# Ten projections turned round: tokens as the stationary operand, 512 columns of weights streaming, and the result turned back by a product with diag(1 / rms)

## The chip, the cores and the metric

The kernel runs on one core of a Trainium2 chip. The metric is the device time of one execution in microseconds (us); smaller is better. Engines: PE is TensorE (its matrix products; PEld is its loading of the stationary operand, which overlaps with them), DVE is VectorE, ACT is ScalarE, POOL is GpSimd, SP is SyncE, whose queue issues nearly all transfers here.

## The reference, cut to what matters

The reference is one block of a flow-matching backbone with two layers on 256 latent tokens (and 256 context tokens) of 2048 channels. Layer 0 mixes tokens with a bidirectional RWKV-7 scan, layer 1 with a Hyena long convolution; after each mixer comes a dense MLP.

```python
for i in range(DEPTH):                       # two layers
    h = modulate(rms_norm(x, norm_g[i, 0]), mod[:, 0], mod[:, 1])
    y = rwkv_mixer(...) if i == 0 else hyena_stream(...)      # last step: ... @ w_o,  ... @ out_w + out_b
    x = x + mod[:, 2] * rms_norm(y, norm_g[i, 1])             # residual 1
    h = modulate(rms_norm(x, norm_g[i, 2]), mod[:, 3], mod[:, 4])
    u = square(relu(h @ mlp_up[i]))                           # 2048 -> 8192
    y = u @ mlp_down[i]                                       # 8192 -> 2048
    x = x + mod[:, 5] * rms_norm(y, norm_g[i, 3])             # residual 2
```

So there are four residuals, and each adds a normalised projection: y times 1 / rms of its token (a number per token), times a gain per channel. The weights that feed them are `w_o` (2048 x 2048), `mlp_down` of layer 0 and of layer 1 (8192 x 2048 each) and `hy_out_w` (2048 x 2048): ten matrices of 2048 x 2048 in all, since the kernel takes `mlp_down` in four parts.

## The kernel before, in words

Activations are held with channels on the 128 partitions and tokens along the row: `x[k]` is 128 channels x 256 tokens, k from 0 to 15. Everything is float32; a product is made from three fp32r products. Each operand is cut into a high part (an ACT cast) and a low part (a DVE subtraction), and `mm3` (lines 158, 159, 160) issues high x high, high x low and low x high into one accumulator in PSUM. In the profile's names `wh`, `wl` are the parts of a weight, `hxh`, `hxl` those of a normalised input of a layer, `uh`, `ul` those of an MLP's hidden values, `yh`, `yl` those of the RWKV mixer's output; `mm` is the accumulator.

`load_split` fetches 1 MB of a weight matrix in one transfer (line 137, queue SP) and cuts it, 1024 columns at a time, with one ACT and one DVE instruction. `gemm_ws` then does a projection with a 128 x 128 block of weights as the stationary operand (the first matrix in a shape such as `128*128 128x256`) and the 256 tokens (258 with two modulation columns) as the moving one. It goes through the output channels two blocks at a time: for each pair, all 16 input blocks k, so 16 x 2 x 3 = 96 products; 8 pairs make 768 products of 256 columns. With `lead=True` the first two pairs run side by side in four accumulators, so that each input block, which is only just being made, is used for four output blocks as soon as it is there.

After a projection `resid` adds it to x. Before, this works on 16 blocks `o[m]` of 128 channels x 256 tokens. While the projection runs, POOL squares each block that comes out and adds it up (`square_sum`, lines 393 to 397). At the end two squares are left to ACT; a product with a matrix of ones sums over the channels (line 370 and 376), ACT takes the root and DVE the reciprocal of a 128 x 256 tile that has the same value in all partitions. Then for each block k: DVE multiplies by gain and 1 / rms into `rt`, DVE (POOL for every fourth block) adds to `x`, ACT scales into `hxh`, DVE makes `hxl`, ACT squares x (`sq`) and PE sums the squares for the next norm (line 376). The next projection (MLP up or Hyena in, both with `lead=True`) consumes `hxh`, `hxl` block by block. The last residual has no next layer: its multiplications and additions are shared between DVE and POOL, and each block goes out by a transfer (line 425).

Beside this the kernel computes the modulation from `ada_w` in the background: transfers into `aw`, and a running sum `acc` made by DVE during the first MLP, by ACT and POOL (line 293) from Hyena on; PE ends each piece with a small product (line 277, `sg<-ones,acc`). A credit counter (`tick`) sets after how many loads of weights such a piece is written into the program. During Hyena's output projection the same counter lets in the spectral part (transposes, `sc` and `sg` products) of the last quarter of the channels, which makes the input blocks 12 to 15 of that projection; the projection's first four output blocks run over k = 0 to 11 beside it, and the counter is drained before k = 12.

The order of instructions on each engine is set at build time by a scheduler that works on the tile dependencies and its own durations; on the chip each engine then runs its list in order. The main loop to keep in mind is this one, for each pair of output blocks:

```python
for k in range(8):
    for i in range(2):
        self.mm3(ps[i][:, :ntok], self.cut(w[k], s), x(k0 + k), ...)   # weights stationary, tokens moving
```

## Time and profile before

| | us |
|---|---|
| median of 3 runs (lowest, highest) | 3775.41 (3771.19, 3782.73) |
| the profiled execution, its own time | 3769.96 |
| its span, first to last instruction | 3768.1 |
| mean granted clock of PE in it | 0.944 |

The stages that the change touches, by the names in the trace: the RWKV output projection from 1523 to 1627 us, the first MLP from 1636 to 2422 us (up and down projections in turn, four of each), Hyena from 2432 us with its output projection from 2832 to 2971 us, the second MLP from 2988 to 3743 us. In the rows below a group reads `line engine operation out<-in shapes xcount | busy us, mean ns | idle before`, and a stretch of time reads, per engine, busy us and the number of instructions, then the granted clock of PE (1.00 is full), the share of the DMA engines in use and the rate in GB/s. A product in the timeline is shown with its start and its modelled duration; products overlap, so their pace is read from start to start.

### The profile page before, as it was taken

How to read it: one execution, taken by the hardware profiler on the slowest of the kernel's cores; microseconds unless marked ns; L12 is line 12 of the kernel's file. 1: busy time of each engine (PE TensorE's matmuls, PEld its weight loads, DVE VectorE, ACT ScalarE, POOL GpSimd, SP SyncE). 2: the span in 40 equal slices, each digit the busy share in tenths (PEclk: the TensorE clock that was granted, in tenths of full speed). 3: DMA queues.
4: the chain of work that ended last, by engine and by line, in shares of the span. 5: the costliest groups of instructions: out<-in, count | busy, mean ns of one | idle time of the engine just before them, and what ended most of it. 6: DMA issues, size and time to landing. Idle time of an engine off the chain costs nothing.

```text
span 3768.1 us, 82300 instructions
## 1 busy us (share of the span) xinstructions
PE 3402.8 (90%) x34206; PEld 3119.8 (83%) x34206; DVE 2513.1 (67%) x3857; ACT 1741.7 (46%) x3045; POOL 684.7 (18%) x706
## 2 busy tenths in 40 slices
PE   7798888888888879889999999899998899999997
PEld 3376677777777767889999999899998799999997
DVE  5887676556566665578776776677787674646554
ACT  4444444443344434444343435465665663534342
POOL 2632221111111100110000001524443730000003
PEclk9899999888888979999999999999999999999998
DMA  9678798887788754668888887566665675656553
GB/s 322 192 229 262 247 314 260 236 237 224 220 236 238 232 149 131 208 207 292 265 276 268 281 266 238 168 216 218 214 218 173 218 232 182 187 182 186 183 184 108
DMA packets 694367, 838.34 MB, mean 222 GB/s; under 512 B 81055, under 2 KB 562240, under 8 KB 693992
## 3 DMA queue, kind: packets, MB, share of 16 engines
q1 hardware_dynamic: 662888, 719.82, 61.1%
q0 software_dynamic: 31104, 113.26, 9.8%
q8 instruction: 268, 4.39, 0.5%
q14 instruction: 107, 0.88, 0.1%
HBM read 778.36 MB, written 54.59 MB: 221 GB/s over the span
## 4 chain that ended last, share of the span: by engine, by line
PE 43%; DMA 15%; DVE 10%; issue 9%; ACT 4%; POOL 3%; SPq 1%; POOLq 0%; ACTq 0%; DVEq 0%
PE mm L158 11%; PE mm L159 11%; PE mm L160 11%; DMA aw<-in_ada_w 7%; PE fl L110 3%; DMA w<-in_mlp_up 2%; DVE wl L53 2%; PE sg L110 2%; PE sc L110 2%; POOL acc L293 2%; DMA sqo<-v 2%; DVE acc L53 1%; DMA fx<-xv 1%; ACT wh L53 1%; ACT aw L53 1%
## 5 line engine op out<-in xcount | busy, mean ns | idle before, releaser
L53 DVE TENSOR_TENSOR wl<-w,wh 128x1024 fp32r<-128x1024 f32 (+1 forms) x716 | 925.4, 1296 | 552.9 <-ACT wh L53 542.4
L53 ACT CAST wh<-w 128x1024 fp32r<-128x1024 f32 (+1 forms) x716 | 741.4, 1044 | 775.7 <-PE mm L159 479.3
L158 PE MATMUL mm<-hxh,wh 128*128 128x258 f32 (+1 forms) x3072 | 873.2, 286 | 23.3 <-ACT hxh L53 18.1
L160 PE MATMUL mm<-hxh,wl 128*128 128x258 f32 (+1 forms) x3072 | 870.7, 285 | 8.7 <-DVE wl L53 8.6
L159 PE MATMUL mm<-hxl,wh 128*128 128x258 f32 (+1 forms) x3072 | 872.1, 284 | 0.2 <-DVE hxl L53 0.2
L158 PEld LDWEIGHTS mm<-hxh,wh 128*128 128x128 f32 x3072 | 582.6, 190 | 26.8 <-ACT hxh L53 19.0
L160 PEld LDWEIGHTS mm<-hxh,wl 128*128 128x128 f32 x3072 | 581.7, 190 | 13.2 <-DVE wl L53 11.6
L159 PEld LDWEIGHTS mm<-hxl,wh 128*128 128x128 f32 x3072 | 584.3, 190 | 3.2 <-DVE hxl L53 1.3
L159 PE MATMUL mm<-ul,wh 128*128 128x256 f32 x2048 | 579.2, 283 | 8.0 <-DVE ul L53 7.8
L158 PE MATMUL mm<-uh,wh 128*128 128x256 f32 x2048 | 578.4, 283 | 5.5 <-ACT uh L53 5.5
L160 PE MATMUL mm<-uh,wl 128*128 128x256 f32 x2048 | 577.9, 282 | 0.0
L293 POOL TENSOR_TENSOR acc<-acc,aw 128x512 f32<-128x512 f32 x180 | 276.5, 1536 | 895.0 <-ACT aw L53 853.1
L159 PEld LDWEIGHTS mm<-ul,wh 128*128 128x128 f32 x2048 | 391.2, 191 | 9.1 <-DVE ul L53 9.1
L158 PEld LDWEIGHTS mm<-uh,wh 128*128 128x128 f32 x2048 | 391.0, 191 | 6.0 <-ACT uh L53 5.9
L160 PEld LDWEIGHTS mm<-uh,wl 128*128 128x128 f32 x2048 | 391.6, 191 | 0.0
L53 DVE SCALAR_TENSOR_TENSOR acc<-aw,sc,acc 128x512 f32<-128x512 f32 x300 | 230.9, 770 | 105.9 <-DMA aw<-in_ada_w 103.3
L110 PE MATMUL fl<-fh,fx 128*128 128x256 f32 x1024 | 233.7, 315 | 21.7 <-DMA fx<-xv 19.9
L110 PEld LDWEIGHTS fl<-fh,fx 128*128 128x128 f32 x1024 | 184.9, 212 | 43.2 <-DMA fx<-xv 24.9
L53 ACT ACTIVATE aw<-aw,sc 128x512 f32<-128x512 f32 x180 | 126.1, 719 | 134.3 <-DMA aw<-in_ada_w 126.8
L53 DVE TENSOR_TENSOR flo<-fr,fh 128x512 fp32r<-128x512 f32 x128 | 87.7, 686 | 124.8 <-ACT fh L53 120.5
L751 POOL DMA_DIRECT2D fx<-xv x128 | 67.9, 530 | 534.4 <-PE fl L110 520.4
L110 PE MATMUL sg<-ard,KB 64*64 64x64 f32 (+1 forms) x3584 | 135.0, 249 | 32.9 <-ACT yf L53 26.0
(351 smaller groups left out, 6203.9 us busy)
## 6 DMA issues: line engine op xcount, KB each, us to landing
aw<-in_ada_w SPq DMA_DIRECT2D x288, 512.0 KB, 5.9
w<-in_mlp_down SPq DMA_DIRECT2D x128, 1024.0 KB, 5.5
w<-in_mlp_up SPq DMA_DIRECT2D x120, 1024.0 KB, 6.3
fx<-xv POOLq DMA_DIRECT2D x128, 512.0 KB, 6.3
aw<-in_ada_w SPq DMA_DIRECT2D x192, 256.0 KB, 3.0
w<-in_hy_in_w SPq DMA_DIRECT2D x44, 1024.0 KB, 5.8
fx<-xr POOLq DMA_DIRECT2D x64, 512.0 KB, 5.5
w<-in_w_k SPq DMA_DIRECT2D x16, 1024.0 KB, 7.8
```

Source lines behind the costliest of these rows:

```text
L53: return self.kern.pin(self.key, f(*a, **kw))
L110: return self.pin("pe", self.nc.tensor.matmul(out, lhsT=lhsT, rhs=rhs, **kw))
L158: nc.tensor.matmul(out, lhsT=wh, rhs=xh, start=first, stop=False)
L159: nc.tensor.matmul(out, lhsT=wh, rhs=xl, start=False, stop=False)
L160: nc.tensor.matmul(out, lhsT=wl, rhs=xh, start=False, stop=last)
L293: nc.gpsimd.tensor_tensor(acc, acc, w[:, a], op=ALU.add)
L751: self.nc.gpsimd.dma_start(x, src)
```

## The change

For the ten projections that feed a residual the operands change places. `gemm_tok` takes a 128 x 128 block of activations (128 input channels x 128 tokens) as the stationary operand and 512 columns of weights as the moving one, so the result has tokens on the partitions: a tile of 128 tokens x 512 channels, for two halves of the tokens and four groups n of channels. The sum of squares over the channels is now a sum along a row, and one ACT instruction (Square with an accumulated sum, `square_rows`) makes it per tile; POOL's squares are gone. `resid` needs 1 / rms only for 128 x 2 numbers. It builds two diagonal matrices `dg` = diag(1 / rms) on DVE, and for each block k two PE products of a stationary y block with `dg` turn the block back to channels x tokens and scale it; they are in full float32 (not fp32r). One DVE instruction then reads this from PSUM, multiplies by the gain and adds to x. Hyena's output bias now varies along the row; it is fetched per group as a 128 x 512 tile `ob`, one buffer, and added by DVE as the accumulator is emptied. In Hyena's output projection the first two groups run side by side over k = 0 to 11 beside the spectral part, in place of the first four output blocks.

```diff
+    def gemm_tok(self, W, x, evac, lead=False, stages=None):
+        for ns in ((0, 1), (2,), (3,)) if lead else ((0,), (1,), (2,), (3,)):
+            ps = {(n, tt): self.mm.tile([P, 512], F32, name="mm") for n in ns for tt in range(2)}
+            for k0 in range(0, KT, 4):
+                if stages and len(ns) > 1:
+                    stages(k0)
+                for n in ns:
+                    w = self.load_split(W[k0 * P : (k0 + 4) * P, n * 512 : (n + 1) * 512].rearrange("(k p) n -> p k n", p=P), 4, 512)
+                    for k in range(k0, k0 + 4):
+                        for tt in range(2):
+                            self.mm3(ps[n, tt], self.cut(x(k), slice(tt * P, (tt + 1) * P)), w[k - k0], k == 0, k == KT - 1)
+                    self.tick(self.rate)
+            for n in ns:
+                for tt in range(2):
+                    evac(n, tt, ps[n, tt])
+
+    def square_rows(self, ss, y, n, tt, pool):
+        t = pool.tile([P, 512], F32, name="ysq", bufs=1)
+        self.nc.scalar.activation(t, y[n, tt], AF.Square, accum_out=ss[:, n, tt : tt + 1])
...
-    def square_sum(self, acc, y, k, pool):
...
-    def resid(self, x, y, acc, layer, gi, ch, pool, nxt=None):
+    def resid(self, x, y, ss, layer, gi, ch, pool, nxt=None):
...
-        r = self.rstd(y[KT - 2 :], self.np, acc)
+        for n in range(1, 4):
+            nc.vector.tensor_tensor(ss[:, 0, :], ss[:, 0, :], ss[:, n, :], op=ALU.add)
+        nc.scalar.activation(ss[:, 1, :], ss[:, 0, :], AF.Sqrt, bias=self.eps[:, 0:1], scale=1.0 / D)
+        nc.vector.reciprocal(ss[:, 1, :], ss[:, 1, :])
+        dg = pool.tile([P, 2, P], F32, name="dg", bufs=1)
+        for tt in range(2):
+            nc.vector.tensor_scalar(dg[:, tt], self.ident, ss[:, 1, tt : tt + 1], None, op0=ALU.mult)
 
         def add(k):
-            t = self.np.tile([P, L], F32, name="rt", bufs=self.RT)
+            pt = self.sg.tile([P, L], F32, name="sg")
+            for tt in range(2):
+                s = slice(tt * P, (tt + 1) * P)
+                nc.tensor.matmul(pt[:, s], lhsT=y[k // 4, tt][:, k % 4 * P : (k % 4 + 1) * P], rhs=dg[:, tt], start=True, stop=True)
+            nc.vector.scalar_tensor_tensor(x[k], pt, gg[:, k : k + 1], x[k], op0=ALU.mult, op1=ALU.add)
             if not nxt:
-                eng = nc.gpsimd if k % 16 in self.LASTP else nc.vector
-                eng.tensor_tensor(t, y[k], r, op=ALU.mult)
-                eng.tensor_tensor(x[k], x[k], t, op=ALU.add)
                 nc.sync.dma_start(self.out[k * P : (k + 1) * P, :], x[k])
                 return
-            nc.vector.scalar_tensor_tensor(t, y[k], gg[:, k : k + 1], r, op0=ALU.mult, op1=ALU.mult)
-            (nc.gpsimd if k % 4 in self.ADDP else nc.vector).tensor_tensor(x[k], x[k], t, op=ALU.add)
             nc.scalar.activation(hi[:, k, :L], x[k], AF.Identity, scale=gs[:, k : k + 1])
...
-            self.gemm_ws(self.I["w_o"][0], D, range(0, KT, 2), lambda k: ys[k], L, ev, True)
+            self.gemm_tok(self.I["w_o"][0], lambda k: ys[k], ev, True)
...
-                self.gemm_ws(I["mlp_down"][layer][D * part : D * part + D], D, range(0, KT, 2), lambda k: u[k], L, evd)
+                self.gemm_tok(I["mlp_down"][layer][D * part : D * part + D], lambda k: u[k], evd)
...
+            def evo(n, tt, ps):
+                if not tt:
+                    bias.append(mp.tile([P, 512], F32, name="ob", bufs=1))
+                    nc.sync.dma_start(bias[n], I["out_b"][:, n * 512 : (n + 1) * 512].broadcast_to([P, 512]))
+                o[n, tt] = yo.tile([P, 512], F32, name="y")
+                nc.vector.tensor_tensor(o[n, tt], ps, bias[n], op=ALU.add)
+                self.square_rows(ss, o, n, tt, mp)
+
+            def come(k0):
+                self.tick(4)
                 if k0 == 12:
                     self.drain()
-                    yh += [split(k) for k in range(12, KT)]
...
+                    yh.extend(split(k) for k in range(12, KT))
+
+            self.gemm_tok(I["hy_out_w"][0], lambda k: yh[k], evo, True, come)
```

The scheduler moves instructions accordingly. Three places matter below. First, PE between the first MLP and Hyena. Before, the last product of the down projection is followed by the sums over the channels, a modulation product (`sg<-ones,acc`), and the first products of the next projection:

```order
L160 MATMUL mm<-uh,wl 128x256
L370 MATMUL sc<-acc,ones 128x256
L277 MATMUL sg<-ones,acc 128x2 x4
L376 MATMUL sc<-sq,ones 128x256 x2
L158 MATMUL mm<-hxh,wh 128x258 x4
L376 MATMUL sc<-sq,ones 128x256 x3
```

Now the products with `dg` (into `sg`, from the y tiles `o_19385` to `o_19392`) stand there; four blocks of them come ahead of the first product of the next projection:

```order
L160 MATMUL mm<-wh,ul 128x512
L443 MATMUL sg<-dg,o_19385 128x128 x2
L443 MATMUL sg<-dg,o_19386 128x128 x2
L443 MATMUL sg<-dg,o_19385 128x128
L443 MATMUL sg<-dg,o_19386 128x128
L443 MATMUL sg<-dg,o_19385 128x128
L443 MATMUL sg<-dg,o_19386 128x128
L158 MATMUL mm<-hxh,wh 128x258 x4
L398 MATMUL sc<-sq,ones 128x256
```

The other twelve blocks are spread between the products of the next projection, each pair next to a product of the squares. Second, DVE in the last residual. Before, it takes the reciprocal of the large tile and then makes several `rt` before it adds them to `x`:

```order
L53 TENSOR_TENSOR o_35231<-o_35231,mm 128x256
L53 RECIPROCAL rstd<-rstd 128x256
L53 TENSOR_TENSOR rt<-o_35216,rstd 128x256
L53 TENSOR_TENSOR rt<-o_35217,rstd 128x256
L53 TENSOR_TENSOR rt<-o_35219,rstd 128x256
L53 TENSOR_TENSOR rt<-o_35220,rstd 128x256
L53 TENSOR_TENSOR x<-x,rt 128x256 x4
```

Now there are a few small instructions and one instruction per block:

```order
L53 TENSOR_TENSOR o_32753<-o_32753,mm 128x512
L53 TENSOR_TENSOR o_32754<-o_32754,mm 128x512
L53 TENSOR_TENSOR ss<-ss 128x2
L53 RECIPROCAL ss<-ss 128x2
L53 TENSOR_SCALAR dg<-ident,ss 128x128 x2
L53 SCALAR_TENSOR_TENSOR x<-sg,gg,x 128x256 x16
```

POOL has no instruction left in this last residual. Third, PE in Hyena's output projection, where the second half of the last spectral part begins with transposes (`sg<-ident,zc`). Before, the projection's products are used up by then, and spectral products stand on both sides:

```order
L159 MATMUL sg<-idftsl,ph 128x256
L160 MATMUL sg<-idftsh,pl 128x256
L1524 MATMUL sg<-ident,zc_33131 128x128
L1524 MATMUL sg<-ident,zc_33141 128x128
L1524 MATMUL sg<-ident,zc_33365 128x128
L1524 MATMUL sg<-ident,zc_33375 128x128
```

Now products of the projection stand between them:

```order
L159 MATMUL mm<-wl,hxh 128x512
L1528 MATMUL sg<-ident,zc_31081 128x128
L1528 MATMUL sg<-ident,zc_31091 128x128
L1528 MATMUL sg<-ident,zc_31314 128x128
L160 MATMUL mm<-wh,hxl 128x512
L158 MATMUL mm<-wh,hxh 128x512
```

The last products of the projection's first twelve input blocks now stand just ahead of the `sc` products of that second half; behind them the rest of the spectral part runs without such company, as before.

80 lines of the change are left out of this document (26 added, 54 removed).

## The prediction

> **What bounds the kernel now.** The page comes first, for the balance of engines.
>
> ```profile
> PE 3402.8 (90%) x34206; PEld 3119.8 (83%) x34206; DVE 2513.1 (67%) x3857; ACT 1741.7 (46%) x3045; POOL 684.7 (18%) x706
> ```
>
> TensorE is busy 90% of the time; that is an average over stages, so the second view is the busy time by stretches. The borders are where the operand names on TensorE change: down projections of the first MLP (parts 0, 1, 2), then part 1 of the second MLP.
>
> ```profile
> core 0: us, PE busy (x) PEld busy (x) DVE busy (x) ACT busy (x) POOL busy (x), PEclk, DMA share, GB/s
> 1742.50:1838.00 95.50, 94.41 (x796) 94.00 (x795) 73.56 (x101) 34.21 (x39) 0.00 (x0) 1.00 0.87 283
> 1934.40:2039.60 105.20, 97.63 (x788) 97.02 (x787) 75.91 (x102) 36.97 (x42) 0.00 (x0) 0.94 0.87 283
> 2134.40:2235.40 101.00, 96.25 (x788) 95.84 (x788) 75.22 (x102) 35.24 (x40) 0.00 (x0) 0.97 0.86 279
> 3284.70:3376.00 91.30, 91.30 (x772) 91.30 (x771) 47.00 (x53) 35.19 (x39) 0.00 (x0) 1.00 0.60 185
> ```
>
> In the second MLP TensorE never pauses and every other engine has room: the pace of the products is the time. In these parts of the first MLP the same 768 products take 95.5, 105.2 and 101.0 us instead of 91.3, with a DMA share of 0.87. So most of the ten projections are bound by the pace of products, three of them partly by something at their start.
>
> **The streaming itself.** The timeline gives the pace: 84 products of 256 columns from the first to the last of these rows, then 48 of 512 columns in an earlier stage.
>
> ```profile
> 3300.06 0.28 PE L158 MATMUL mm<-uh,wh 128*128 128x256 f32 x1
> ...
> 3309.91 0.28 PE L160 MATMUL mm<-uh,wl 128*128 128x256 f32 x1
> ```
>
> ```profile
> 213.81 0.40 PE L158 MATMUL mm<-xh,wh 128*128 128x512 f32 x1
> ...
> 224.48 0.40 PE L160 MATMUL mm<-xh,wl 128*128 128x512 f32 x1
> ```
>
> 9.85 us / 83 steps = 118.7 ns, and 10.67 us / 47 = 227.0 ns. Two points give 0.423 ns a column and some 10.4 ns per product. The change makes one 512-column product out of two 256-column ones: 384 for 768 in each of the ten projections. Gain: 3840 x (2 x 118.7 - 227.0) = 3840 x 10.4 ns = 40 us. Loads and splits stay the same in bytes and number (16 loads of 1 MB, 32 splits); they are wanted every 24 x 0.227 = 5.45 us instead of 48 x 0.1187 = 5.70 us. Lower bound: if all stages outside the second MLP gain nothing, four projections remain, 16 us. I take 40, since outside their stalls the slower stages run at the same pace.
>
> The Trainium skill (TensorE: Matmul & The Clock Gate, Back-to-back issue gap) gives a warm gap of N / 2.4 + 2.5 ns, with only 2.5 ns per product to be saved: 109.2 ns for 256 and 215.8 for 512 columns, so 3840 x 2.5 = 10 us in this sum instead of 40. The rows above disagree with it at both widths.
>
> **Starts of the down projections.** The view of waits for the first 40 us of part 1, then of part 2:
>
> ```profile
> ACT wh L53 <- DMA w<-in_mlp_down: 5.2, 2, 2.8
> PE mm L158 <- ACT uh L53: 4.5, 1, 4.5
> PE mm L159 <- DVE ul L53: 3.1, 1, 3.1
> ```
>
> ```profile
> PE mm L159 <- DVE ul L53: 3.7, 1, 3.7
> ```
>
> TensorE reaches the last hidden blocks (k = 14, 15) before they are made: 7.6 us of waiting in part 1, and then the clock falls (0.94 over 105.2 us is 6.3 us lost; together 13.9, the whole excess over 91.3). Part 2 has 9.7 us of excess, part 0 4.2: 28 us in all. The block k = 14 is wanted after 14/16 of the first column group: 84 x 0.1187 = 10 us after the start before, 84 x 0.227 = 19 us now. 9 us is more than the waits, so they go, and the clock stays up. But a load that ACT waits for (5.2 us) is late too, and will be wanted 5% sooner. Bounds: 28 and 0; I take 12, somewhat below the middle, since the DMA share there is already 0.87.
>
> **The three residuals with a next layer.** The stretches from the last product of a projection to the first evacuation of the next one's leading group (RWKV to MLP, MLP to Hyena, Hyena to MLP), and the last residual:
>
> ```profile
> 1626.60:1670.70 44.10, 33.67 (x231) 31.38 (x229) 39.97 (x70) 21.85 (x45) 5.03 (x4) 0.88 0.63 198
> 2421.80:2470.60 48.80, 37.11 (x238) 34.05 (x237) 42.94 (x62) 32.27 (x63) 23.05 (x17) 0.86 0.58 179
> 2971.50:3029.90 58.40, 39.26 (x252) 35.15 (x252) 44.59 (x57) 36.85 (x71) 34.25 (x27) 0.85 0.61 190
> 3742.70:3768.10 25.40, 1.53 (x6) 0.67 (x5) 14.93 (x25) 2.03 (x5) 8.15 (x10) 0.57 0.25 83
> ```
>
> DVE is the busy one (40 of 44 us, 43 of 49), and its list is in an unlucky order:
>
> ```profile
> 2426.56 3.55 DVE L53 SCALAR_TENSOR_TENSOR rt<-o,gg,rstd 128x256 f32<-128x256 f32 x5
> 2430.04 1.42 DVE L53 TENSOR_TENSOR x<-x,rt 128x256 f32<-128x256 f32 x4
> 2438.63 1.50 DVE L53 TENSOR_TENSOR x<-x,rt 128x256 f32<-128x256 f32 x1
> ```
>
> Five multiplications come ahead of the first addition, which so starts 3.5 us late, and an addition can take 1.50 us. So TensorE begins the next projection late: 9.8 us after the last product ahead of Hyena, 16.1 us ahead of the second MLP:
>
> ```profile
> 2431.62 0.58 PE L158 MATMUL mm<-hxh,wh 128*128 128x258 f32 x1 [7.39 <-ACT hxh L53]
> ...
> 2987.64 0.58 PE L158 MATMUL mm<-hxh,wh 128*128 128x258 f32 x1 [3.67 <-ACT hxh L53]
> ```
>  Prices for the new chain, from groups of like instructions (512 columns from PSUM on DVE; 512 on ACT; 256 from PSUM; the low part; a tiny one on ACT):
>
> ```profile
> L53 DVE TENSOR_TENSOR hf<-sg,win 128x512 f32<-128x512 f32 x32 | 21.7, 688 | 26.6 <-PE sg L160 23.7 <-DMA win<-in_window 2.8
> L53 ACT ACTIVATE aw<-aw,sc 128x512 f32<-128x512 f32 x180 | 126.1, 719 | 134.3 <-DMA aw<-in_ada_w 126.8 <-POOL acc L293 3.7 <-POOL acc L397 3.4
> L53 DVE TENSOR_TENSOR nt<-mm,rstd 128x256 f32<-128x256 f32 x128 | 53.3, 418 | 13.6 <-ACT ns L53 13.5
> L53 DVE SCALAR_TENSOR_TENSOR hxl<-x,gs,hxh 128x256 fp32r<-128x256 f32 x48 | 33.8, 729 | 0.0
> L53 ACT COPY ns<-mm 128x1 f32<-128x1 f32 x128 | 19.6, 155 | 44.8 <-PE mm L160 44.7
> ```
>
> A full-precision product is read from the sums of squares, between products of the next projection:
>
> ```profile
> 2994.04 0.59 PE L376 MATMUL sc<-sq,ones 128*128 128x256 f32 x2
> 2994.28 0.47 PE L158 MATMUL mm<-hxh,wh 128*128 128x258 f32 x1
> 2994.59 0.38 PE L376 MATMUL sc<-sq,ones 128*128 128x256 f32 x1
> ```
>
> From one to the next is 0.55 us for it and one product of 0.12, so 0.43 us for 256 columns and, by columns, some 0.21 for the 128 of a `dg` product. The new chain after the last product: evacuation 0.69, square 0.72, then a sum, a root, a reciprocal (two columns each, 0.15 to 0.25) and two diagonals (about 0.25 each), 1.0 to 1.3 together, first `dg` products 0.43 and their way through: 3.5 us to the first block in PSUM, against these 9.8 to 16.1 us. Then TensorE has, per block, 12 x 0.12 + 0.43 (sum of squares) + 0.43 (two `dg` products) = 2.3 us, 16 x 2.3 = 37 us; DVE has 0.42 + 0.47 to 0.73, plus half a split, 1.5 to 1.8 us, ACT about 1.4. So TensorE takes over as the bound, with 3.5 + 37, some 2 us of low clock and some 1.5 of handing over: 44 us for each of the three, against 44.1, 48.8 and 58.4. The third holds waits for POOL's `acc`, which I expect to shrink only in part (POOL loses its squares, not the modulation): 48 rather than 44. Sum 0 + 5 + 10 = 15 us; I take 10, for 48 hand-overs of PE to DVE through two `sg` buffers. Bounds: gain 20, loss 8 (half a microsecond more per hand-over).
>
> **The last residual.** No next layer, no split:
>
> ```profile
> 3746.75 3.01 DVE L53 TENSOR_TENSOR rt<-o,rstd 128x256 f32<-128x256 f32 x4
> 3748.64 11.99 SPq L425 DMA_DIRECT2D out<-x  x16
> 3758.41 1.08 DVE L53 TENSOR_TENSOR x<-x,rt 128x256 f32<-128x256 f32 x3
> ```
>
> Before, the last block is done 3759.5 - 3742.7 = 16.8 us after the last product. Now 3.5 us, then 16 blocks at the pace of two `dg` products or one DVE instruction: 0.43 us each at full clock (10.4 us in all), 0.86 at half (17.3). The row above has the mean clock at 0.57. Gain between 6.4 and -0.5: I take 3.5.
>
> **Hyena's output projection.** The spectral part of the last quarter beside the projection, then without it:
>
> ```profile
> 2831.90:2859.50 27.60, 25.91 (x187) 23.98 (x188) 27.39 (x37) 17.43 (x31) 8.38 (x7) 1.00 0.62 189
> 2859.50:2890.70 31.20, 23.89 (x118) 19.28 (x117) 19.14 (x34) 6.25 (x11) 0.00 (x0) 0.84 0.22 70
> ```
>
> In the second row 118 spectral products (16 us at 0.12 to 0.23 each) take 31.2 us, since nothing fills their gaps. The cover of k = 0 to 11 grows from 144 x 0.119 = 17 us to 144 x 0.227 = 33 us (the same share of the work in later groups is saved), and by the new order it reaches past the transposes, leaving 72 of the 118. Of 15 us lost about 6 come back; bounds 10 and 0. Against this the bias: the tile `ob` of group 1 can only be fetched once group 0 has been emptied, and SP's queue stands at it until then (the loads behind it have no free buffer earlier). DVE, with splits queued behind, waits for it: about 2 us, the landing time of a transfer of the same 256 KB; bounds 0 and twice that, 4.
>
> ```profile
> spec<-ko SPq DMA_DIRECT2D x32, 256.0 KB, 2.0
> ```
>
> So the net gain is 4.
>
> **Sum.** 40 + 12 + 10 + 3.5 + 4 = 69.5 us off the profiled execution's 3770.0 (span 3768.1, 1.9 us around it): 3700.5. That execution was 5.4 us below the median of the runs (3775.4), so the median to expect is 3706 us.
>
> **Rivals.**
>
> The loads set the pace in the first MLP. For it: a share of 0.87 and waits for `w`; against it: part 0 comes within 4.2 us of full pace at the same share. Then 16 + 0 + 10 + 3.5 + 2 = 31.5 us: 3744.
>
> The residuals don't gain, because the `dg` products and hand-overs on TensorE eat what DVE saves. For it: 37 us of work where 30 stood; against: the idle time and low clock before. Then 40 + 12 - 8 + 0 + 4 = 48: 3727.
>
> The starts lose all their waiting and the residuals gain their whole 20: 40 + 28 + 20 + 6 + 6 = 100: 3675.
>
> A fixed part of 2.5 ns per product, with the rest of the 10.4 growing with columns: 69.5 - 30 = 39.5, 3736. The 47 steps at 227 ns speak against it. (It is the rule of the Trainium skill cited above.)
>
> Slower: the hand-over from PE through `sg` to DVE. TensorE runs its list in order, so if DVE is held by POOL (1.50 us for an addition, above) in both of its instructions per block, TensorE stands with it. It costs 2 x 1.0 us for each of 48 blocks, 96 us, against a rest of 59.5: 3812. It decides from 1.25 us more per block on. POOL is busy in 5, 23 and 34 us of the three stretches, and the mean of the low part is 0.73 us, not 1.5: unlikely.
>
> That the change doesn't do what it says can be left out: its order has half the products, with 512 columns.
>
> **How the numbers follow.** Forecast 3706: 0.52 (its own range, 3692 to 3722). Loads 3744: 0.15. No gain in the residuals 3727: 0.16. The larger gain 3675: 0.10. The fixed part 3736: 0.03. Slower: 0.03. Nothing either way: 0.01. The range that holds 8 in 10 reaches from 3668 to 3745. A change under 0.3% (11 us) can't be told from none: all cases but the last two are beyond it, so faster 0.95, same 0.02, slower 0.03.
>
> **What would show it.** Streaming: a part of the second MLP's down projection in 87.2 us, products 0.227 apart, TensorE without a pause. Starts: parts 1 and 2 of the first MLP near 90 us, no wait for `uh` or `ul`, clock at 1.00. Residuals: first product of the next projection 4 to 6 us after the last one, stretches of 44, 44 and 48 us. Last residual: 13 us to the last block. Hyena: its output projection in about 131 us instead of 139.6, with one wait of DVE for `ob`. The forecast is wrong if the products come at 0.235 us or more, if ACT waits for `w` through the first MLP, or if TensorE waits for DVE in each block.

## The result, and the profile after

The changed kernel takes 3723.3 us (median of four runs, 3709.7 to 3735.9) against 3773.7 us for the kernel before (3771.2 to 3782.7): ratio 0.986, 95% interval 0.981 to 0.991. It is faster, by 50 us where 70 were forecast; the time lies inside the range and 17 us above the forecast. The profiled execution of the changed kernel took 3713.0 us, 57 us less than the profiled one of before.

The page of the changed kernel begins:

```profile
PE 3377.0 (91%) x30598; PEld 2932.6 (79%) x30598; DVE 2474.0 (67%) x3771; ACT 1745.0 (47%) x3069; POOL 555.5 (15%) x576
```

TensorE has 3608 instructions fewer (34206 before) but only 26 us less busy time. The busy time by stretches shows where the 57 us come from. The borders are the same places of the program in both: the RWKV output projection; from its last product to the end of the last up projection of the first MLP (seven projections and a residual); the last down projection of that MLP; the residual and Hyena's input part; Hyena's output projection; the residual and the second MLP; the last residual. First the kernel before (its last residual is shown in the prediction), then the changed one:

```profile
core 0: us, PE busy (x) PEld busy (x) DVE busy (x) ACT busy (x) POOL busy (x), PEclk, DMA share, GB/s
1523.30:1626.60 103.30, 97.39 (x769) 96.69 (x770) 55.48 (x65) 39.14 (x48) 24.99 (x27) 0.95 0.64 199
1626.60:2330.10 703.50, 677.79 (x5543) 673.55 (x5542) 534.11 (x780) 296.28 (x450) 6.33 (x5) 0.98 0.83 266
2330.10:2421.80 91.70, 91.57 (x771) 91.36 (x770) 52.77 (x54) 40.78 (x53) 51.43 (x43) 1.00 0.64 202
2421.80:2831.90 410.10, 381.77 (x2881) 365.60 (x2879) 323.89 (x430) 254.37 (x422) 160.00 (x149) 0.97 0.66 210
2831.90:2971.50 139.60, 126.97 (x939) 119.35 (x939) 92.73 (x101) 74.11 (x112) 77.40 (x58) 0.96 0.63 201
2971.50:3742.70 771.20, 752.06 (x6212) 747.95 (x6213) 445.78 (x558) 358.67 (x533) 80.68 (x68) 0.99 0.59 183
```

```profile
1515.60:1612.00 96.40, 91.62 (x384) 73.68 (x384) 49.97 (x58) 43.21 (x60) 0.00 (x0) 0.96 0.63 207
1612.00:2310.50 698.50, 674.17 (x4450) 618.42 (x4450) 525.53 (x747) 292.50 (x449) 0.00 (x0) 0.99 0.82 267
2310.50:2399.20 88.70, 88.67 (x386) 71.86 (x384) 50.89 (x47) 46.50 (x67) 24.92 (x17) 1.00 0.65 211
2399.20:2809.30 410.10, 385.66 (x2945) 371.43 (x2945) 319.85 (x420) 255.02 (x425) 156.99 (x145) 0.98 0.66 211
2809.30:2934.30 125.00, 118.18 (x546) 95.16 (x544) 89.16 (x111) 66.20 (x99) 33.59 (x23) 0.99 0.63 210
2934.30:3692.60 758.30, 746.84 (x4736) 678.76 (x4736) 436.05 (x520) 363.04 (x540) 64.60 (x44) 0.99 0.59 189
3692.60:3711.20 18.60, 11.26 (x65) 9.62 (x64) 9.17 (x22) 1.74 (x5) 0.00 (x0) 0.89 0.34 114
```

| place | before | after | gained | forecast there |
|---|---|---|---|---|
| RWKV output projection | 103.3 | 96.4 | 6.9 | 4 (streaming) |
| first residual, first MLP to its last up | 703.5 | 698.5 | 5.0 | 24 (streaming 12, starts 12) |
| its last down | 91.7 | 88.7 | 3.0 | 4 |
| second residual, Hyena's input | 410.1 | 410.1 | 0.0 | 3 of the 10 for residuals |
| Hyena's output projection | 139.6 | 125.0 | 14.6 | 8 (streaming 4, net 4) |
| third residual, second MLP | 771.2 | 758.3 | 12.9 | 23 (streaming 16, residual 7) |
| last residual | 25.4 | 18.6 | 6.8 | 3.5 |

That is 49.2 us. The other 7.7 us lie ahead of the first changed product (1523.3 against 1515.6 us from the span's start), where nothing was changed. In five more profiles of kernels that are alike up to there (the unchanged copy and the runs with the 256 columns, the unused bytes, the single group and the late pieces, all below) it came between 1509.9 and 1523.7 us. So 7.7 us is within the scatter of that part, and stages are compared one by one here, not by their place in the span.

The large miss is the second row of the table: seven projections of the first MLP move the same bytes at the same rate, 703.5 us at 266 GB/s and 698.5 us at 267. (One expectation below gives 701.7 us for before; it ends the stretch 1.8 us ahead of the first product of the last down projection.) In the changed kernel, its copy and three runs below with the same first MLP (the unused bytes, the single group, the late pieces) this stretch takes 693.6 to 703.5 us. Against one profile of before, a gain of 5.0 us there can't be told from none.

### The profile page after: what moved, and what is told of

It is laid out like the page before. It is cut to its first block, busy times and chain, and to the rows that moved or that the text cites. A ratio compares the mean times of both kernels' runs of the same rounds, so it can differ in the third digit from the quotient of the medians.

```text
span 3711.2 us, 74689 instructions
## 1 busy us (share of the span) xinstructions
PE 3377.0 (91%) x30598; PEld 2932.6 (79%) x30598; DVE 2474.0 (67%) x3771; ACT 1745.0 (47%) x3069; POOL 555.5 (15%) x576
## 4 chain that ended last, share of the span: by engine, by line
PE 50%; DMA 20%; DVE 11%; issue 10%; ACT 5%; POOL 3%; SPq 1%; POOLq 0%; ACTq 0%; DVEq 0%
PE mm L158 12%; PE mm L160 12%; PE mm L159 12%; DMA aw<-in_ada_w 9%; PE fl L110 3%; DVE wl L53 2%; PE sg L110 2%; PE sc L110 2%; DMA w<-in_mlp_down 2%; POOL acc L315 2%; DVE acc L53 2%; ACT wh L53 1%; DMA fx<-xv 1%; DMA sqo<-v 1%; DMA w<-in_mlp_up 1%
## 5 line engine op out<-in xcount | busy, mean ns | idle before, releaser
L158 PE MATMUL mm<-hxh,wh 128*128 128x258 f32 x2816 | 803.5, 286 | 15.8 <-DVE nt L53 13.4
L160 PE MATMUL mm<-hxh,wl 128*128 128x258 f32 x2816 | 803.8, 286 | 6.6 <-DVE wl L53 6.4
L159 PE MATMUL mm<-hxl,wh 128*128 128x258 f32 x2816 | 800.2, 284 | 0.0
L158 PE MATMUL mm<-wh,uh 128*128 128x512 f32 x1024 | 405.3, 396 | 0.4 <-DVE nt L53 0.4
L159 PE MATMUL mm<-wl,uh 128*128 128x512 f32 x1024 | 400.5, 391 | 4.4 <-DVE wl L53 4.4
L160 PE MATMUL mm<-wh,ul 128*128 128x512 f32 x1024 | 402.3, 393 | 0.0
L110 PE MATMUL fl<-fh,fx 128*128 128x256 f32 x1024 | 227.0, 309 | 14.0 <-DMA fx<-xv 12.5
L159 PEld LDWEIGHTS mm<-wl,uh 128*128 128x128 f32 x1024 | 192.3, 188 | 51.3 <-DVE wl L53 8.5
L160 PEld LDWEIGHTS mm<-wh,ul 128*128 128x128 f32 x1024 | 192.1, 188 | 45.6
L158 PEld LDWEIGHTS mm<-wh,uh 128*128 128x128 f32 x1024 | 192.3, 188 | 41.5 <-DVE nt L53 0.8
L110 PE MATMUL fl<-flo,fx 128*128 128x256 f32 x512 | 152.5, 298 | 0.8 <-DVE flo L53 0.8
```

Of the source, the lines that this page charges most:

```text
L110: return self.pin("pe", self.nc.tensor.matmul(out, lhsT=lhsT, rhs=rhs, **kw))
L158: nc.tensor.matmul(out, lhsT=wh, rhs=xh, start=first, stop=False)
L159: nc.tensor.matmul(out, lhsT=wh, rhs=xl, start=False, stop=False)
L160: nc.tensor.matmul(out, lhsT=wl, rhs=xh, start=False, stop=last)
```

## The experiments

Every ratio is to the kernel before, run beside it on the same chip, since chips differ (medians of before: 3761 to 3778 us).

**The changed kernel again.**

> The changed kernel once more, unchanged, so that the experiments of this call stand beside it on the same chip. Its four executions so far lie in two groups, 3710 to 3713 us and 3734 to 3736 us, against 3774 us for the kernel before. If the two groups are a property of each execution, the median comes out anywhere between 3710 and 3736; if they belonged to the chip, all executions here would lie in one group.

3721.8 us, ratio 0.986 (0.984 to 0.989), single times 3711.6, 3718.1, 3725.5 and 3726.8: no two groups, only a scatter of some 15 us. Its profile has the same table: 703.5, 88.6, 410.6, 126.4 us for rows two to five. From the first changed product to the end it takes 2203.8 us, the first profile of the changed kernel 2195.6, before 2244.8.

**Streaming alone.** Each product of 512 columns as two of 256:

```diff
-self.mm3(ps[n, tt], self.cut(x(k), ...), w[k - k0], k == 0, k == KT - 1)
+for h in (slice(0, L), slice(L, 2 * L)):
+    self.mm3(ps[n, tt][:, h], self.cut(x(k), ...), self.cut(w[k - k0], h), ...)
```

> The changed kernel, but each product of 512 columns in the five tokens-first projections is issued as two of 256 columns: tokens stay on the parts, residuals, loads and splits stay as they are. This prices the streaming alone. By the rows of the changed kernel (230.4 ns a product of 512 in the MLPs against 2 x 118.7 before) it costs 3840 x 7.0 = 27 us, 16 us if the four down projections of the first MLP hide it behind other waits: 3738 to 3749 where the changed kernel has 3722. By the prediction's figure (10.4 ns saved per pair) it costs 40 us: 3762. By a fixed part of 2.5 ns it costs 10: 3732.

3724.5 us, ratio 0.989 (0.987 to 0.992), 0.0031 above the changed kernel's 0.9863 (0.984 to 0.989): 12 us, but the intervals overlap. The profiles tell more: from the first changed product on it takes 2211.6 us, where the changed kernel, its copy and the three runs named with them above take 2192.3 to 2203.8. So the width is worth 8 to 19 us, not 40. The 12 lie nearest to the smallest figure of the expectation, but not by its way. The rows: the last down projection of the second MLP, and Hyena's output projection.

```profile
3614.70:3706.20 91.50, 91.50 (x770) 91.32 (x768) 39.77 (x42) 33.84 (x44) 0.00 (x0) 1.00 0.41 132
2815.90:2936.20 120.30, 117.00 (x926) 113.16 (x924) 82.52 (x109) 55.73 (x80) 8.34 (x6) 1.00 0.55 182
```

In the second MLP a projection in narrow products takes 91.5 us where the wide ones take 88.7: 2.8 us a projection. In Hyena, where spectral products go in between, the narrow ones are faster, 120.3 against 125.0 and 126.4: there the width costs 5 to 6 us. The first MLP's stretch takes 703.7 us with narrow products, against the 693.6 to 703.5 above, so no price shows there. The wide products pay where nothing else wants TensorE; in Hyena they cost.

**Where the tiles lie.** 2.8 us is less than the 4 forecast, since a step is not 227 ns everywhere. Rows of the changed kernel's timeline, 48 products apart: the RWKV output projection, then the last down projection of the second MLP.

```profile
1569.71 0.39 PE L158 MATMUL mm<-wh,yh 128*128 128x512 f32 x1
...
1580.59 0.39 PE L158 MATMUL mm<-wh,yh 128*128 128x512 f32 x1
```

```profile
3626.04 0.40 PE L158 MATMUL mm<-wh,uh 128*128 128x512 f32 x1
...
3637.10 0.40 PE L158 MATMUL mm<-wh,uh 128*128 128x512 f32 x1
```

10.88 / 48 = 226.7 ns and 11.06 / 48 = 230.4 ns, at full clock and without a wait. The tiles lie at other addresses, so an unused tile was put ahead of the MLP's:

```diff
+self.pool(es, "pad").tile([P, 184], F32, name="pad")
 mp, mu = self.pool(es, "mp"), self.pool(es, "mu", 16)
```

> The changed kernel with 736 unused bytes per partition ahead of the MLP's tiles, so that hidden blocks and weights start at multiples of 1024 bytes instead of 288 bytes above one. In the changed kernel a product of 512 columns takes 226.9 ns in the RWKV output projection (tiles 96 bytes above a multiple of 1024), 230.4 in the MLPs (288 above) and 232.5 in Hyena (672 and others). Theory 'place': the step falls to 227 in the eight down projections, 3072 x 3.5 ns = 11 us: 3711 where the changed kernel has 3722. Theory 'place plays no part': the steps stay at 230 to 231 and the time within 5 us of 3722.

3711.7 us, ratio 0.986 (0.983 to 0.989), no difference from the changed kernel. (It is the time that 'place' foretold, but on a chip where the kernel before takes 3762 us instead of 3774.) The same projection takes

```profile
3607.70:3697.00 89.30, 89.30 (x386) 71.98 (x384) 39.77 (x42) 33.87 (x45) 0.00 (x0) 1.00 0.40 134
```

89.3 us instead of 88.7, 232 ns a step; the other profiles of wide products have 88.7 or 88.8 again, so this is no scatter. Nothing else was changed, so the place of the tiles does move the step, but the even boundary made it longer, not 227. Whether another place would give 227 in the MLPs stays open; over the eight down projections that would be 3072 x 3.7 ns, some 11 us.

**The first MLP.** The waits of ACT and TensorE that tell most in the 700 us of the second row (us in total, times, longest), first before, then after:

```profile
ACT wh L53 <- DMA w<-in_mlp_up: 118.4, 29, 10.9
ACT wh L53 <- PE mm L159: 94.9, 56, 7.6
...
ACT wh L53 <- DMA w<-in_mlp_down: 48.5, 15, 6.3
...
ACT wh L53 <- PE mm L160: 16.3, 4, 7.6
...
PE mm L159 <- DVE ul L53: 7.8, 3, 3.7
...
PE mm L158 <- ACT hxh L53: 7.0, 1, 7.0
...
PE mm L158 <- ACT uh L53: 5.5, 2, 4.5
...
PE mm L158 <- DVE nt L53: 4.1, 3, 2.2
```

```profile
ACT wh L53 <- DMA w<-in_mlp_up: 125.8, 27, 12.0
ACT wh L53 <- DMA w<-in_mlp_down: 123.0, 24, 10.8
...
PE mm L158 <- DVE nt L53: 11.9, 9, 2.9
...
PE mm L159 <- DVE wl L53: 4.4, 8, 1.0
```

The waits for `uh` and `ul` are gone, as forecast. But ACT, which before waited 111 us (94.9 and 16.3) for buffers that TensorE had to free, now waits 249 us for weights instead of 167, and TensorE waits longer for evacuations (`nt`) and for low parts of weights (`wl`). The evacuations stand on DVE behind work on late weights. Ahead of the longest wait (2.9 us, at 2040.7) ACT had waited 9.7 us for weights and DVE 5.3 us for a modulation piece (`aw`); then DVE made three sums and a split before it came to the evacuation. All of TensorE's waits in the stretch come to 25.6 us before and 24.1 after. Moving four of the sixteen pieces of modulation weights out of this stage tells whether the bytes matter, in both kernels:

```diff
-ADA = (4, 8, 16, 8, 4)
+ADA = (4, 8, 12, 12, 4)
```

> The changed kernel with four of the sixteen pieces of modulation weights (4 x 4.2 MB) moved out of the first MLP into the Hyena stage. In the changed kernel the first MLP takes 778 us for about 214 MB, 275 GB/s, while in the second MLP an up and a down projection take 92.4 and 88.6 us. Theory 'loads': the first MLP is held by its transfers as a whole, and the waits that left the starts of the down projections came back in the next up projections for that reason. Then 197 MB at 280 GB/s are 704 us, TensorE becomes the bound with 4 x 92.4 + 4 x 88.6 + 15 for the residual in its lead = 739 us, and the first MLP loses 30 to 40 us; Hyena gets 64 more additions on POOL and gives back 0 to 15. Time 3683 to 3708 where the unchanged kernel has 3723. Theory 'starts': the waits belong to the change from one projection to the next, whatever the loads do; only DVE is relieved (64 x 0.77 us off its list), the first MLP moves by less than 8 us, time 3713 to 3723.

> The kernel before with the same move of four pieces of modulation weights out of the first MLP. Theory 'loads': its waits for the last hidden blocks come from weights that are late; the first MLP goes from 785 us to about 4 x 92.4 + 4 x 91.3 + 15 = 750, time 3739 to 3755, and the change is worth 45 to 55 us with this move as without it. Theory of the prediction (TensorE reaches the last hidden blocks too early by its own pace): at least 20 of the 28 us of waiting stay, time 3760 to 3774, and the change is then worth some 20 us more with this move than without.

3829.6 us for the changed kernel (ratio 1.015, 1.012 to 1.018) and 3866.5 for the one before (1.025, 1.023 to 1.027); with the move the change is worth 37 us, without it 53 on this chip. (By the rows of the result the first MLP moves 205 MB at 261 GB/s, not the 214 and 275 of the first expectation.) The same stretch of seven projections, first after, then before, and Hyena's output projection after:

```profile
1624.20:2302.50 678.30, 665.45 (x4411) 614.19 (x4411) 484.59 (x679) 296.54 (x451) 0.00 (x0) 0.99 0.77 250
2841.80:3060.80 219.00, 155.83 (x698) 126.43 (x696) 112.52 (x138) 98.17 (x146) 87.35 (x63) 0.84 0.55 176
```

```profile
1623.00:2304.00 681.00, 666.46 (x5505) 663.01 (x5504) 493.10 (x711) 298.09 (x449) 7.21 (x4) 0.99 0.78 249
```

With 17 MB fewer (678.3 us x 250 GB/s against 698.5 x 267) the stretch loses 20 us after and 22.5 before, so both were held by what these pieces bring: half of the loads theory is right. Both expectations missed the price in Hyena: in the changed kernel 93 us in the output projection, where the pieces pile up in the last quarter, and 39 us in the input part (449.9 against 410.6). And the change is worth 2.7 us in this stretch with fewer pieces, 5.0 with all of them. Three down projections at 2.6 us each should give 7.8; the first residual, ahead of them, gives back 5.9 (44.1 us before, 50.0 after, below). So the pieces hold the 700 us in both kernels, but a relief from them does not make the change gain more there.

Is it the bytes, or DVE's work on the pieces? The sums were given to ACT and POOL, with the bytes left where they were:

```diff
-ONP = (False, False, False, True, True)
+ONP = (False, False, True, True, True)
```

> The changed kernel with the modulation sums of the first MLP taken from DVE (256 operations of 0.77 us, 197 us) and given to ACT (256 x 0.72 us) and POOL (240 x 1.5 us), as the later stages do; the loads stay. Moving four pieces out of the first MLP took 24 us off it, from 783 to 759. If those came from the transfers, nothing changes here or it gets worse, because POOL holds DVE's splits (1.94 instead of 1.23 us where both work): first MLP 783 to 810 us, time 3722 to 3750. If they came from DVE's list, the first MLP falls to 755 to 768 us, time 3695 to 3708.

3753.9 us, ratio 0.998 (0.996 to 0.999), worse than the changed kernel by 1.2%, and beyond what either theory allowed. The stretch goes to 741.5 us,

```profile
1604.70:2346.20 741.50, 689.40 (x4450) 625.50 (x4450) 493.76 (x491) 454.36 (x706) 377.97 (x240) 0.98 0.78 252
```

with ACT busy for 454 us instead of 293. This does not single out the transfers, since ACT makes the high parts of all weights. Nor does it clear DVE: 256 instructions (747 against 491), about 190 us of work, left it, but its busy time fell only from 525.5 to 493.8 us, because what stayed took longer beside POOL's additions, a low part of the weights 1598 ns on average instead of 1220. ACT's waits for weights fell from 249 to 87 us while the stretch grew by 43, so these waits alone are no measure of the time. Whether bytes or DVE's work hold the stretch stays open.

Moved into the scan instead, or spread over the whole stage:

```diff
-ADA = (4, 8, 16, 8, 4)
+ADA = (4, 12, 12, 8, 4)
```

> The changed kernel with four of the sixteen pieces of modulation weights (16.8 MB) moved out of the first MLP into the scan of the first stage, where TensorE multiplies them, and Hyena left as it is. Moved to Hyena, the same pieces took 24 us off the first MLP and cost 93 us in Hyena's output projection; given to POOL within the first MLP they cost it 38. Theory 'the first MLP is held by its transfers and the splits that wait for them': it falls again from 783 to 755 to 762 us. If the scan hides the 128 products of 256 columns and the transfers, the time falls by 20 to 28 us to about 3697 (ratio to before 0.979 to 0.981); if the scan, whose list is in a fixed order, gets them on its path, it gives back 10 to 50 us (ratio 0.983 to 0.993).

```diff
-self.bg, self.rate = [ada], self.ADA[2 + i] * 8 / 108
+self.bg, self.rate = [ada], self.ADA[2 + i] * 8 / (108 if i else 126)
```

> The changed kernel with the sixteen pieces of modulation weights of the first MLP spread over all of its 128 weight loads, where they are now done after some 110 of them (8/126 of a piece per load instead of 8/108); nothing leaves the stage. From the residual to the end of the last up projection both kernels move the same bytes at the same rate: 701.7 us at 266 GB/s before, 698.5 us at 267 after, and the last down projection, without pieces, runs at its own 88.7 us. Theory 'the transfers set these 700 us': 13% fewer pieces fall into them (some 10 of 186 MB), so they shrink by 15 to 25 us, and the last down projection stays within 4 us of 89; time 3697 to 3710 where the changed kernel has 3722 (ratio to before 0.980 to 0.983). Theory 'the pieces' work on DVE or the order of the list sets them': no more than 6 us, ratio 0.985 to 0.987.

3766.2 us (ratio 1.001, 0.999 to 1.003) and 3732.8 us (0.988, 0.986 to 0.990). In the scan run the stretch takes 675.4 us. The rows of the spread run: the stretch, the last down projection and the two parts of Hyena.

```profile
1613.50:2296.20 682.70, 669.03 (x4426) 616.74 (x4426) 510.09 (x721) 293.18 (x447) 0.00 (x0) 0.99 0.81 265
2296.20:2386.40 90.20, 90.20 (x400) 73.50 (x398) 57.32 (x72) 37.04 (x52) 0.13 (x2) 1.00 0.66 221
...
2386.40:2804.20 417.80, 383.67 (x2890) 368.16 (x2890) 303.47 (x417) 258.03 (x431) 159.95 (x148) 0.98 0.65 210
2804.20:2948.00 143.80, 130.58 (x609) 105.07 (x608) 94.50 (x114) 74.44 (x111) 53.55 (x35) 0.96 0.63 207
```

Four kernels, four times the stretch fell (by 20, 22.5, 23 and 16 us), and each time another stage gave back more: the scan about 69 us (the first changed product behind it starts at 1588.5 instead of 1519.9 us), Hyena's output projection 93 (219.0 against 126.4; in the kernel before 96, 235.9 against 139.6), and even with the mere spread Hyena takes 25 us more (417.8 + 143.8 against 410.6 + 126.4). The likely reason in that last case, which no run tests by itself, is a start that was not in sight: POOL's sums for Hyena. The group of POOL's additions, in the unchanged copy and in the spread run (minimum, median and longest ns; first and last start):

```profile
L315 POOL TENSOR_TENSOR acc<-acc,aw x180: 1263/1346/2362, 2319.0 to 3056.3; 128x512 f32<-128x512 f32 x180
```

```profile
L315 POOL TENSOR_TENSOR acc<-acc,aw x180: 1262/1348/3255, 2430.8 to 3065.6; 128x512 f32<-128x512 f32 x180
```

In the changed kernel Hyena's pieces start 90 us ahead of Hyena (2408.6), under the last down projection, where the first MLP has no pieces of its own left; spread out, the first MLP's own pieces hold that place and Hyena's begin 44 us after its start (2386.4).

**The residuals.** The residual block read by DVE without the products that turn it (with the chain of sums kept):

```diff
-for tt in range(2):
-    nc.tensor.matmul(pt[:, s], lhsT=y[k // 4, tt][...], rhs=dg[:, tt], start=True, stop=True)
-nc.vector.scalar_tensor_tensor(x[k], pt, gg[:, k : k + 1], x[k], ...)
+nc.vector.tensor_scalar(gg, gg, ss[:, 1, 0:1], None, op0=ALU.mult)    # once, ahead of add
...
+y3 = y[k // 4, 0][:, k % 2 * L : (k % 2 + 1) * L]
+nc.vector.scalar_tensor_tensor(x[k], y3, gg[:, k : k + 1], x[k], ...)
```

> The changed kernel without the products that turn the projection back: each residual block is read from the untransposed tile by DVE, after the same chain of sums of squares, root and diagonals (left out: the 32 products with the diagonal in each of the four residuals and their way through PSUM; the scaling uses one value per partition). Theory 'TensorE sets the pace of the residuals': the 16 x 0.43 us of products go from each, and the four stretches (50.0, 43.5, 54.3 and 18.6 us) lose 4 to 7 us each, 16 to 28 us together: time 3695 to 3707 where the unchanged kernel has 3723. Theory 'the chain behind the last product and the hand-over to DVE and ACT set it': the stretches move by under 2 us each, time 3715 to 3723.

3718.4 us, ratio 0.986 (0.984 to 0.988), no difference that can be told. The three stretches of the changed kernel, then all four without the turn:

```profile
1612.00:1662.00 50.00, 40.55 (x298) 39.08 (x297) 39.13 (x70) 25.51 (x52) 0.00 (x0) 0.93 0.70 222
2399.20:2442.70 43.50, 39.83 (x297) 38.68 (x297) 27.52 (x50) 24.72 (x52) 0.00 (x0) 0.96 0.43 137
2934.30:2988.60 54.30, 42.85 (x304) 40.89 (x304) 33.76 (x48) 36.94 (x70) 27.45 (x20) 0.91 0.69 215
```

```profile
1619.00:1664.10 45.10, 32.63 (x225) 30.16 (x225) 34.13 (x63) 24.87 (x52) 0.00 (x0) 0.92 0.66 212
2403.10:2451.90 48.80, 36.34 (x233) 32.77 (x231) 32.16 (x54) 32.42 (x65) 23.78 (x13) 0.90 0.64 202
2942.10:2997.30 55.20, 37.82 (x241) 34.76 (x239) 32.33 (x50) 35.61 (x70) 32.38 (x20) 0.81 0.69 215
3703.70:3717.50 13.80, 0.00 (x0) 0.00 (x0) 8.05 (x22) 1.74 (x5) 0.00 (x0) 0.67 0.46 152
```

The first stretch loses 5 us and the last residual 5, as 'TensorE sets the pace' asked; the second gains 5 and the third 1. Neither theory holds for all four. In the second, POOL is busy for 24 us where it did nothing before: the order without the turn let Hyena's sums in, so that case is not a clean one.

What the changed kernel's first three stretches have in common is a late start. Its timeline behind the last product of the first of them (1612.0 us):

```profile
1612.73 1.04 ACT L53 CAST wh<-w 128x1024 fp32r<-128x1024 f32 x1 [1.79 <-DMA w<-in_mlp_up]
1613.68 0.63 ACT L53 ACTIVATE ysq<-o 128x512 f32<-128x512 f32 x1
...
1615.17 1.28 ACT L53 ACT_TABLE_LOAD   x1
...
1616.46 0.30 ACT L53 ACTIVATE ss<-ss,eps 128x2 f32<-128x2 f32 x1
...
1617.33 1.01 PE L443 MATMUL sg<-dg,o 128*128 128x128 f32 x3 [5.30 <-DVE dg L53]
```

The squares stand in ACT's queue behind a split for the next projection, and the root behind the loading of its table. The first product with the diagonal comes 5.3 us after the last one here, and 3.6 and 8.7 us in the other two. The third has no table to load, but ahead of the root ACT has two splits and four steps of the modulation beside the squares, and DVE's sum of 128 x 2 numbers takes 1.22 us beside POOL's additions, where it takes 0.16 us here.

**Hyena's output projection.** One group beside the spectral part, then the pieces called as late as before:

```diff
-for ns in ((0, 1), (2,), (3,)) if lead else ((0,), (1,), (2,), (3,)):
+for ns in ((0, 1), (2,), (3,)) if lead and not stages else ((0,), (1,), (2,), (3,)):
...
-if stages and len(ns) > 1:
+if stages and ns[0] == 0:
```

> The changed kernel, but Hyena's output projection starts with one column group beside the spectral part instead of two. Theory 'cover': half of the cover (96 products of 0.23 us) is gone, and what fell from 139.6 us before to 125 to 126.4 us comes back in good part: the projection takes 133 to 140 us and the time is 3729 to 3736. Theory 'not the cover' (the old order with its eight and four blocks of k was the cause): it stays within 3 us of 126 and the time at 3722 to 3725.

```diff
+self.rate = 0.0
 def come(k0):
-    self.tick(4)
+    if k0:
+        self.tick(8)
```

> The changed kernel, but the spectral pieces of Hyena's last quarter are called as late in its output projection as in the kernel before: none ahead of the first four blocks of k, eight ahead of each of the next two, none between. With one column group or two beside it the projection took 125.6 and 126.4 us, against 139.6 before, so the number of covering products did not decide. Theory 'when the pieces come': before, the last spectral products ran 89 us after the projection's first product, in the changed kernel 69 us; called late they end 80 to 90 us after it again and the projection takes 134 to 140 us, 3730 to 3736 where the changed kernel has 3722 (ratio to before 0.988 to 0.990). Theory 'the rest of the change' (evacuations, bias, half the products): it stays within 4 us of 126, ratio 0.986 to 0.987.

3711.8 us (ratio 0.986, 0.984 to 0.989) and 3713.4 us (0.986, 0.984 to 0.989), the projection in 125.6 and 126.5 us. No effect from either, and neither edit did what it was meant to, since the instruction order is made by a scheduler. With one group, spectral products run between those of the second group, and only 32 instead of 72 stand alone at the end; so that edit did not take the cover away. With the late call the spectral products stand in nearly the same places as in the unchanged copy, the last one 67.2 and 67.9 us after the projection's first product. The figure of 89 against 69 us, on which the second expectation rests, was mine and is wrong: it set the projection's start before 30 us too early (it is 59 us before, 67 after). What the cover may have done stands in the changed kernel's trace, in the stretch where spectral products run alone (its counterpart is the 31.2 us in the prediction):

```profile
2858.50:2876.00 17.50, 13.37 (x70) 10.72 (x69) 13.59 (x23) 3.81 (x8) 0.00 (x0) 0.90 0.24 84
```

**The spread and narrow products in Hyena together**, the one candidate for a faster version:

> The version before this one (modulation weights spread over the whole first MLP), and Hyena's output projection alone in products of 256 columns, as in the run with 256 columns everywhere, where that projection took 120.3 us instead of 126.4. If the two gains add, it is 6 us faster than the version with the spread alone; if Hyena's 6 us came from elsewhere, there is no difference beyond 2 us.

3730.1 us, ratio 0.986 (0.984 to 0.989) on the chip where the spread alone had 0.988 (0.986 to 0.990): 3 us by the medians, 8 by the ratios, within the scatter. In the traces Hyena's output projection takes 142.0 us against 143.8, so the 6 us were not to be had behind the late sums. No version that was run can be told to beat the changed kernel.

## Why the prediction was right, and where it was not

That the kernel gets faster was right; four of the terms were wrong in size, and one step failed.

*Streaming, 40 us.* The mechanism (half as many products save a fixed part of each) is right, the term was mis-sized: the second MLP's last down projection takes 88.7 us instead of 91.3, not 87.2. The 227.0 ns came from another stage, and in the MLPs the step is 230.4 ns. That is 2.6 us a projection and 26 us over ten, if all gave it; Hyena's share has the other sign, and in the first MLP's stretch none shows. The run with 256 columns prices the whole at 12 us, 8 to 19 by the profiles. On the warning that the prediction cited (the Trainium skill, TensorE: Matmul & The Clock Gate, Back-to-back issue gap; 10 us in this sum): at 512 columns the rows have 226.7 and 230.4 ns where that rule, which the page gives for an isolated product, has 215.8, so it stays refuted as a figure for these products. That its 10 us are nearer to the net price than 40 is luck, since the second MLP saves 2.6 us a projection, and not 1.

*Starts, 12 us.* This is the step that failed. "9 us is more than the waits, so they go, and the clock stays up" came true, word for word: no wait for `uh` or `ul`, a clock of 1.00 in the down projections of the first MLP. The three down projections did lose 22 us, where 24 were forecast for width and starts together: 95.5, 105.2 and 101.0 us became 91.3, 94.3 and 94.0. The step took for granted that the rest of the stage would stay as it was, and it gave 17 us back: the two up projections behind parts 1 and 2 rose from 94.2 and 94.9 us to 101.8 and 100.4, and the first residual with its up projection from 115.9 to 120.9 (the one behind part 0 fell by 1). The longest of TensorE's waits there begins with late transfers, as shown above; whether the bytes or DVE's work hold the stage, no run separates. The 28 us of excess were misread too: the rows of the prediction have 796, 788 and 788 products against 772, and those 56 more, for the modulation, are work and not waiting, some 6 us by the spread run's last down projection (14 more products, 1.5 us). The prediction had named ACT's waits for `w` as the sign that it is wrong, and they grew from 167 to 249 us. The rival in which the loads set the pace described this stage (it gave nothing for it), though not the total, 3744.

*Three residuals, 10 us.* Gained: -5.9, 5.3 and 4.1, so 3.5 in place of 10. From the first diagonal product to the end of the stretch it is 44.7, 40.0 and 45.6 us, against 37 us of work and 3.5 of loss: right in the second, 4 to 5 us over in the others. Wrong too was the chain ahead of it, 3.1 us up to the first diagonal product, measured at 5.3, 3.6 and 8.7: the terms left out are ACT's queue, a table of 1.28 us in the first, and in the third DVE beside POOL. So the first product of the next projection came 9.3, 7.3 and 12.6 us after the last one, not 4 to 6. That TensorE is the bound there is not shown: taking away its 7 us gave 5 in one of three. The 5.3 us of the second residual are not seen in the end, since Hyena's input takes as much longer.

*Last residual, 3.5 us.* Measured 6.8, over the upper bound of 6.4, but only 2.0 of it on the path forecast: the last block is done 14.8 us after the last product, before 16.8, and 13 were forecast. The clock, which had stood at 0.57, is 0.89 with the diagonal products. Most of the rest lies behind the last transfer. Waits of POOL's sequencer at the end of the program, before and after (shortest, median and longest ns; first and last start):

```profile
L1754 POOLq DRAIN  x3: 40/102/10757, 3756.5 to 3767.8; - x3
```

```profile
L1760 POOLq DRAIN  x2: 40/66/93, 3710.7 to 3711.0; - x2
```

Before, POOL works in this residual until 3758.2 us, and its wait lasts until 3767.3, 4.6 us after the last entry of the SP queue that it then answers (3762.7); in the changed kernel it has nothing to do there and answers at once. Why the wait is so long is not shown. The prediction had no term for it, so this part of the gain is luck.

*Hyena, net 4.* "Leaving 72 of the 118" spectral products without cover: 70 are left. But the stretch fell from 31.2 to 17.5 us, by 13.7, and not by the 6 that I let come back of 15. In the order of the instructions the cover came as forecast; its worth did not. The wait of DVE for `ob` is there, once, 2.9 us against the 2 assumed, and TensorE shows no wait for it:

```profile
DVE y L53 <- DMA ob<-in_out_b: 2.9, 1, 2.9
```

That the cover is the cause is not shown: it rests on these rows alone, the two runs that were to test it did not take it away, and with one group the uncovered part was shorter still at the same time for the whole.

So 49 us came where 70 were forecast: 20 too much were put on the first MLP with its residual, 10 on the second, 3 on Hyena's input; Hyena's output projection, the last residual and RWKV's output projection gave 13 more than forecast. That the total came out no further off is in part luck: misses of 33 us on one side met 13 on the other, and nearly 5 of these come from the end of the program.

## What to carry to other kernels

A stall that goes from one projection may only move to the next: before costing it as a gain, compare bytes moved and time over the whole stage, and ask which queue waits for transfers once the stall is gone. Work that is moved or spread out falls on another stage, and may take the slot in which the next stage's work had started early, so measure a relief to the end of the kernel, not to the end of its stage. Where a scheduler makes the order, look in the trace whether an edit has moved what it was meant to move. And a chain that is short in instructions is as long as the queues in which its links stand.

## What the runs showed of the hardware

The step of back-to-back products with 512 columns in the same program, at full clock and without waits, is 226.7 ns in one stage and 230.4 in another, and moving the tiles of the second by 736 bytes made it 232. At 256 columns the same product takes 119.1 ns a step with tokens stationary (91.5 us / 768). The diagonal products kept the clock up: 0.89 over the last residual, against 0.57 before and 0.67 without them. At the program's end a wait of POOL's sequencer lasted 10.8 us where POOL had worked in the last residual (in this profile of the kernel before and in its run with the moved pieces), and 0.1 us where it had not.
